# Second layer of a two-layer trunk: four of eight weight pairs with seven products in the first groups of chunks 1 and 2, and four of their banks copied aside

## The chip, the cores and the metric

The kernel runs on one core of one Trainium2 chip. The metric is the device time of one execution, in microseconds; times of several runs are given as their median. TensorE is called PE here, VectorE DVE, ScalarE ACT, GpSimd POOL, and SP is the engine that issues the loads.

## What is computed

256 tokens of width 2048 pass two layers. Each layer has attention (chunked in the first, stick-breaking in the second), a cross-attention into 256 memory tokens, an output projection, and a squared-ReLU MLP with 8192 inner features. The change is in the second layer's MLP. Of the reference this matters:

```
def sq_relu_mlp(h, g, w_in, w_out):
    return jnp.square(jax.nn.relu(rms_norm(h, g) @ w_in)) @ w_out

h = h + sq_relu_mlp(h, norm_mlp[layer], w_mlp_in[layer], w_mlp_out[layer])
```

## The kernel before

All products are made in three passes of a reduced-precision float: every operand is split into a high part `hi` and a low part `lo`, and hi*hi, hi*lo and lo*hi are summed in a PSUM bank. Weights stream from HBM in units of 128 x 1024 float32 (512 KB). SP loads a unit into `raw`; ACT casts `raw` to `hi`; DVE subtracts to get `lo`; then PE may use it. `weights()` keeps up to three units prepared ahead of the one that PE takes (`AHEAD = 3`, four `hi` and five `lo` buffers).

The MLP of a layer goes through the 8192 features in four chunks `c` of 2048 (`NCH = 4`). A chunk has two stages. The **up projection** makes the 2048 activated features of the chunk, 16 tiles of 128 features, two at a time (`two_tiles`, `up`, `finish`); DVE works on each tile after PE. The **down projection** multiplies them with the weights of the chunk and adds to sums over chunks. For chunks 0, 1 and 2 it has two groups, `pair_group(c, 0, ...)` and `pair_group(c, 1, ...)`; each makes 1024 of the 2048 output columns for both halves of the tokens, as four blocks of 128 x 512 that are called 11, 21, 12 and 22 (token half, column half).

A group goes through eight pairs of k-tiles, `j` = 0 to 7. A pair is done in one of two ways:
- with **eight products**: two units, step "1" for the column half 1 and step "2" for half 2; each is 12 matmuls of 512 columns, into banks 11 and 21, or 12 and 22. Together 24 matmuls, two casts, two subtractions.
- with **seven products** (a Strassen-Winograd scheme; `Sevenfold`, `prepare_seven`): steps 0 to 3 with 6, 3, 6 and 6 matmuls, together 21, into the four banks and four more, p1, p5, p6 and p7. Its weights are sums of the four blocks of a pair, which DVE makes in place in `raw` (steps 2 and 3: lines 222, 223, 225 and 226, each 512 wide), and every step has a cast (line 227) and a subtraction (line 228) of its own, 1024 wide except in step 1, which is 512 wide. The activations for it (`factors`, tiles `s12`, `s34`, `s_hi`, `s_lo`) are made in the up projection.

The table `SEVEN[layer][chunk][group]` lists which pairs use seven products: THREE is 0, 2, 4 and FOUR is 0, 2, 4, 6. `group_order` puts the units of the other pairs between the steps of the sevens: behind steps 1, 2 and 3 for THREE, behind steps 1 and 2 for FOUR.

When a bank is complete, `add` adds it to sums in SBUF: `d` tiles hold the four blocks of each group summed over chunks, `e` tiles the sums for p1 and p6, for p5, and for p7. Bank p1 goes into two sums, each other bank into one, so a group has nine additions of 512 columns. They are done in one of three ways: DVE adds from the bank (line 1042), ACT copies a bank that starts a sum (line 1040, chunk 0), or, where a list `staged` is given, ACT copies the bank to SBUF (line 1035) and DVE adds the copy later (line 1143). Before the change `staged` is given in the second groups of chunks 1 and 2, and in the first group of chunk 3.

PE runs its instructions in the order of the code. The other engines' instructions are put in an order by a scheduler when the kernel is built, and each engine then runs in that order, waiting at an instruction until its inputs are there.

Of the kernel before, what the change touches and what calls it, by code (L numbers as in the profile page):

```python
# [9 lines left out]
F32 = mybir.dt.float32  # L10
# [6 lines left out]
P = 128  # L17
# [7 lines left out]
NCH = FF // D  # L25
# [20 lines left out]
THREE, FOUR = (0, 2, 4), (0, 2, 4, 6)  # L46
SEVEN = [
    [(FOUR, FOUR), (THREE, FOUR), (THREE, FOUR), (THREE,)],
    [(FOUR, FOUR), (THREE, FOUR), (THREE, FOUR), (FOUR,)],
]  # L50


def group_order(sevens):


    others = [(j, col) for col in "12" for j in range(KT // 2) if j not in sevens]
    behind = (1, 2, 3) if len(sevens) == 3 else (1, 2)
    steps = []
    for j in sevens:
        for i in range(4):  # L60
            steps.append((j, i))
            if i in behind:
                steps.append(others.pop(0))
    return steps + others
# [41 lines left out]
def trunk(  # L106
# [25 lines left out]
    wide = ctx.enter_context(tc.tile_pool(name="wide", bufs=7))  # L132
# [124 lines left out]
    def weights(held=0):  # L257

        while len(prepared) < AHEAD + 1 - held and state["next"] < len(stream):
            prepare()  # L260
        return prepared.popleft()
# [6 lines left out]
    def start_side(g):  # L268
        active.append(g)
# [4 lines left out]
    def slot():  # L274
        clock["slot"] += 1
        if waiting and clock["slot"] >= max(clock["last"] + waiting[0][1], waiting[0][2]):
            active.append(waiting.popleft()[0])
            clock["last"] = clock["slot"]
        for g in list(active):
            try:  # L280
                next(g)
            except StopIteration:
                active.remove(g)
# [326 lines left out]
    def heads4(name):  # L610
        return grp.tile([P, 1024], F32, name=name, tag="g4")
# [139 lines left out]
    def new_act(name):  # L751
        return acts.tile([P, KT, 2 * T], F32R, name=name, tag="act")
# [203 lines left out]
    def mlp(l, xg_, sq, h, done):  # L956
# [4 lines left out]
        def summed(m, g):  # L961

            return sums[2 * m + g // 2][:, (g % 2) * 512 : (g % 2 + 1) * 512]
# [3 lines left out]
        def product_sum(i, n):  # L967

            return extra[i][:, n * 512 : (n + 1) * 512]

        def turned(g, then):

            for o in (4 * g, 4 * g + 2):
                yield
                tp = ps_t.tile([P, 512], F32, name="tp", tag="t")
                for i in range(2):
                    for m in range(2):
                        a = (o + i - 4 * g) * P
                        nc.tensor.transpose(
                            tp[:, i * T + m * P : i * T + (m + 1) * P],  # L980
                            summed(m, g)[:, a : a + P], ident[:],
                        )
                nc.vector.tensor_tensor(h(o, 2), tp[:], h(o, 2), op=ALU.add)  # L983
                if then is not None:
                    then(o)
                    then(o + 1)

        def merged(n):

            u, p5, p7 = (product_sum(i, n) for i in range(3))  # L990
            for i, (dst, src) in enumerate((
                (summed(0, 2 * n + 1), u),
                (summed(0, 2 * n + 1), p5),
                (u, p7),
                (summed(1, 2 * n), u),
                (u, p5),
                (summed(1, 2 * n + 1), u),
            )):
                nc.vector.tensor_tensor(dst, dst, src, op=ALU.add)
                if i % 2 == 1:  # L1000
                    yield

        def product(bank, a, w, count):

            for lhs, rhs in ((a[0], w[0]), (a[0], w[1]), (a[1], w[0])):
                mm(bank[:], lhs, rhs, count[0] == 0, count[0] == count[1] - 1)
                count[0] += 1

        def pair_group(c, n, hid, factors, staged=None):

            banks = {q: ps_mm.tile([P, 512], F32, name="acc", tag="acc") for q in ("11", "21", "12", "22")}
            banks.update((q, ps_s.tile([P, 512], F32, name="acc", tag="s")) for q in ("p1", "p5"))
            banks["p6"] = ps_t.tile([P, 512], F32, name="acc", tag="t")
            banks["p7"] = ps_y.tile([P, 512], F32, name="acc", tag="y")
            sevens = len(SEVEN[l][c][n])
            counts = {q: [0, 3 * sevens] for q in banks}
            for q in ("11", "21", "12", "22"):
                counts[q][1] = 6 * (KT // 2 - sevens) + (3 * sevens if q != "22" else 0)

            sums_of = {  # L1020
                "11": [summed(0, 2 * n)], "21": [summed(1, 2 * n)],
                "12": [summed(0, 2 * n + 1)], "22": [summed(1, 2 * n + 1)],
                "p1": [product_sum(0, n), summed(0, 2 * n)], "p6": [product_sum(0, n)],
                "p5": [product_sum(1, n)], "p7": [product_sum(2, n)],
            }

            def add(q, a, w):
                product(banks[q], a, w, counts[q])
                if counts[q][0] < counts[q][1]:
                    return  # L1030
                src = banks[q][:]
                if staged is not None and q in ("12", "22", "p1", "p5", "p6", "p7"):

                    copy = wide.tile([P, 512], F32, name="copy", tag="wide")
                    nc.scalar.copy(copy[:], src)
                    staged.extend((dst, copy[:]) for dst in sums_of[q])
                    return
                for dst in sums_of[q]:
                    if c == 0 and q not in ("11", "p6"):
                        nc.scalar.copy(dst, src)  # L1040
                    else:
                        nc.vector.tensor_tensor(dst, src, dst, op=ALU.add)

            def tokens(kt, m):
                return [hid[:, kt, i * T + m * P : i * T + (m + 1) * P] for i in range(2)]

            def part(unit, k2):
                return [x[:, k2 * 512 : (k2 + 1) * 512] for x in unit]

            for j, step in group_order(SEVEN[l][c][n]):  # L1050
                w = weights()
                if step in ("1", "2"):
                    for m in range(2):
                        for k2 in range(2):
                            add(f"{m + 1}{step}", tokens(2 * j + k2, m), part(w, k2))
                    slot()
                    continue
                s = factors[j]
                pairs = [
                    (("p1", tokens(2 * j, 0)), ("11", tokens(2 * j + 1, 0))),  # L1060
                    (("12", s[3]),),
                    (("p5", s[0]), ("p7", s[2])),
                    (("p6", s[1]), ("21", tokens(2 * j + 1, 1))),
                ][step]
                for k2, (q, a) in enumerate(pairs):
                    add(q, a, part(w, k2))
                if step in (1, 3):
                    slot()

        began = clock["slot"]  # L1070
        for c in range(NCH):
            hid = new_act(f"hid{l}_{c}")
            squares = {}
            factors = {}
# [56 lines left out]
            n = FIRST_UP if c == 0 else 0  # L1131
# [2 lines left out]
                two_tiles(xg_, [lambda b, i=i: up(i, b) for i in (f, f + 1)])  # L1134

            if c < NCH - 1:
                pair_group(c, 0, hid, factors)
                staged = None if c == 0 else []
                pair_group(c, 1, hid, factors, staged)

                def add_second(staged=staged, c=c):
                    for i, (dst, src) in enumerate(staged or ()):
                        nc.vector.tensor_tensor(dst, dst, src, op=ALU.add)
                        if i % 2 == 1:
                            yield
                    if c == NCH - 2:
                        yield from merged(1)
                        if l == 1:
                            yield from turned(3, None)

                start_side(add_second())
                continue

            staged = [] if l == 1 else None
# [21 lines left out]
            def down_early(o, bank):  # L1176
                low = low_part(bank)
                nc.gpsimd.tensor_tensor(low[:], low[:], h(o), op=ALU.add)
                nc.vector.tensor_tensor(h(o), bank[:, :T], low[:], op=ALU.add)
# [12 lines left out]
            for g in range(2, 4):  # L1192
# [3 lines left out]
                for o in range(4 * g, 4 * g + 4):  # L1196
                    if o == KT - 1:
                        last_tile(
                            hid, lambda b, o=o: down_early(o, b), lambda b, o=o: down_last(o, b)
# [97 lines left out]
    for hd in range(NH):  # L1297
        q = nar.tile([P, T], F32, name=f"qb{hd}", tag="bias", bufs=6)
# [83 lines left out]
```

## Time and profile before

| | |
|---|---|
| median of 3 runs | 2172.17 us (2171.57 to 2173.44) |
| the profiled execution, own time | 2173.2 us |
| its span in the trace | 2171.3 us |
| busy in the span | PE 2164.1, DVE 1639.0, ACT 1196.6, POOL 324.4 us |

The span is the time from the program's first instruction to its last one in the trace; the execution's own time is 1.9 us more. Busy time is the sum over an engine's instructions without overlap. A matmul's shown duration is longer than the time until the next one starts, because they are pipelined: what counts is the distance between starts. The same holds on DVE, where the next instruction starts a little before the shown end of the last.

### The profile page before, as it was taken

How to read it: one execution, taken by the hardware profiler on the slowest of the kernel's cores; microseconds unless marked ns; L12 is line 12 of the kernel's file. 1: busy time of each engine (PE TensorE's matmuls, PEld its weight loads, DVE VectorE, ACT ScalarE, POOL GpSimd, SP SyncE). 2: the span in 40 equal slices, each digit the busy share in tenths (PEclk: the TensorE clock that was granted, in tenths of full speed). 3: DMA queues.
4: the chain of work that ended last, by engine and by line, in shares of the span. 5: the costliest groups of instructions: out<-in, count | busy, mean ns of one | idle time of the engine just before them, and what ended most of it. 6: DMA issues, size and time to landing. Idle time of an engine off the chain costs nothing.

```text
span 2171.3 us, 30203 instructions
## 1 busy us (share of the span) xinstructions
PE 2164.1 (100%) x11123; PEld 1856.6 (86%) x11123; DVE 1639.0 (75%) x2239; ACT 1196.6 (55%) x1680; POOL 324.4 (15%) x349
## 2 busy tenths in 40 slices
PE   9999999999999999999999999999999999999999
PEld 8888888888888888888878888888888888888887
DVE  7765555677977987997876556567797798799796
ACT  7645545555655565555545447655565556555553
POOL 0010102621001001001041112253100100100100
PEclk9999999999999999999999999999999999999999
DMA  9655656665765765666666654455676567667664
GB/s 331 194 173 162 180 173 196 187 193 168 210 214 172 210 210 184 192 214 192 200 177 186 182 192 140 130 185 184 181 207 216 172 198 221 191 178 221 187 182 155
DMA packets 213315, 414.64 MB, mean 191 GB/s; under 512 B 13232, under 2 KB 144304, under 8 KB 213168
## 3 DMA queue, kind: packets, MB, share of 16 engines
q1 hardware_dynamic: 212592, 410.63, 62.3%
q8 instruction: 87, 1.43, 0.3%
q10 hardware_dynamic: 576, 2.10, 0.3%
q14 instruction: 60, 0.49, 0.1%
HBM read 410.58 MB, written 2.10 MB: 190 GB/s over the span
## 4 chain that ended last, share of the span: by engine, by line
PE 99%; DVE 0%; DMA 0%; ACT 0%; issue 0%; ACTq 0%
PE acc L77 94%; PE accs L77 1%; PE tp L77 1%; PE yp L77 1%; PE s L77 1%; PE z L77 1%; DMA raw<-in_w_o 0%; PE cold L77 0%; ACT hi L173 0%; DVE lo L250 0%; DVE h L983 0%; DVE lo L176 0%; DVE kvx L465 0%; ACT hi L249 0%; PE stat L77 0%
## 5 line engine op out<-in xcount | busy, mean ns | idle before, releaser
L176 DVE TENSOR_TENSOR lo<-raw,hi 128x1024 fp32r<-128x1024 f32 (+1 forms) x524 | 644.4, 1237 | 357.6 <-ACT hi L173 239.5
L173 ACT CAST hi<-raw 128x1024 fp32r<-128x1024 f32 (+1 forms) x524 | 546.7, 1045 | 380.0 <-PE acc L77 307.5
L77 PE MATMUL acc<-hi,hid 128*128 128x512 f32 x1474 | 482.4, 390 | 0.0
L77 PE MATMUL acc<-mlpx,hi 128*128 128x512 f32 x2048 | 472.6, 390 | 0.0
L77 PEld LDWEIGHTS acc<-mlpx,hi 128*128 128x128 f32 x2048 | 382.0, 188 | 77.8
L77 PEld LDWEIGHTS acc<-hi,hid 128*128 128x128 f32 x1474 | 277.4, 188 | 57.7
L77 PE MATMUL acc<-lo,hid 128*128 128x512 f32 x737 | 287.4, 390 | 0.0
L1080 POOL TENSOR_TENSOR hid<-upsq,hid 128x256 fp32r<-128x256 f32 x128 | 122.2, 963 | 1086.2 <-ACT hid L1079 1086.2
L227 ACT CAST hi<-raw 128x1024 fp32r<-128x1024 f32 x204 | 192.0, 946 | 132.8 <-PE acc L77 57.2
L77 PEld LDWEIGHTS acc<-mlpx,lo 128*128 128x128 f32 x2048 | 250.6, 192 | 2.8
L77 PE MATMUL acc<-mlpx,lo 128*128 128x256 f32 x2048 | 252.0, 283 | 0.0
L228 DVE TENSOR_TENSOR lo<-raw,hi 128x1024 fp32r<-128x1024 f32 x204 | 222.8, 1107 | 29.3 <-ACT hi L227 27.7
L249 ACT CAST hi<-raw 128x1024 fp32r<-128x1024 f32 x146 | 154.0, 1055 | 127.5 <-PE acc L77 104.0
L77 PE MATMUL acc<-hi,xg 128*128 128x512 f32 x640 | 210.5, 399 | 0.0
L250 DVE TENSOR_TENSOR lo<-raw,hi 128x1024 fp32r<-128x1024 f32 x146 | 178.4, 1222 | 16.3 <-ACT hi L249 15.6
L77 PEld LDWEIGHTS acc<-lo,hid 128*128 128x128 f32 x737 | 138.7, 188 | 28.7
L77 PEld LDWEIGHTS acc<-hi,xg 128*128 128x128 f32 x640 | 120.2, 188 | 24.6
L451 ACT COPY low<-acc 128x256 f32<-128x256 f32 x188 | 69.1, 368 | 112.5 <-PE acc L77 112.2
L77 PE MATMUL acc<-lo,xg 128*128 128x512 f32 x320 | 124.7, 390 | 0.0
L77 PE MATMUL acc<-y,hi 128*128 128x512 f32 x512 | 119.9, 391 | 0.0
L77 PEld LDWEIGHTS acc<-y,hi 128*128 128x128 f32 x512 | 95.0, 188 | 19.1
L1079 ACT CAST hid<-upsq 128x256 fp32r<-128x256 f32 x128 | 51.9, 406 | 77.1 <-DVE upsq L1078 77.1
(200 smaller groups left out, 2570.5 us busy)
## 6 DMA issues: line engine op xcount, KB each, us to landing
raw<-in_w_up SPq DMA_DIRECT2D x256, 512.0 KB, 4.4
raw<-in_w_down SPq DMA_DIRECT2D x256, 512.0 KB, 5.6
raw<-in_w_in SPq DMA_DIRECT2D x80, 512.0 KB, 3.6
raw<-in_w_o SPq DMA_DIRECT2D x64, 512.0 KB, 3.9
raw<-in_w_mem SPq DMA_DIRECT2D x28, 512.0 KB, 6.2
raw<-in_w_kv_v SPq DMA_DIRECT2D x24, 512.0 KB, 3.7
raw<-in_w_kv_k SPq DMA_DIRECT2D x24, 512.0 KB, 4.0
raw<-in_w_q SPq DMA_DIRECT2D x24, 512.0 KB, 4.2
```

Of the source, the lines that this page charges most:

```text
L77: return self._tc.keep_in_program_order(fn(*args, **kwargs))
L173: nc.scalar.copy(hi[:, :n], raw[:, :n])
L176: nc.vector.tensor_tensor(lo, raw, hi.bitcast(F32), op=ALU.subtract)
L227: nc.scalar.copy(hi4, src)
L228: nc.vector.tensor_tensor(lo4, src, hi4.bitcast(F32), op=ALU.subtract)
L249: nc.scalar.copy(hi4, turned)
L250: nc.vector.tensor_tensor(lo4, turned, hi4.bitcast(F32), op=ALU.subtract)
L451: nc.scalar.copy(low[:], bank[:, T:])
L1079: nc.scalar.copy(hid[:, f, :T], a[:])
L1080: nc.gpsimd.tensor_tensor(hid[:, f, T:], a[:], hid[:, f, :T].bitcast(F32), op=ALU.subtract)
```

## The change

In the second layer the first groups of chunks 1 and 2 use four sevens, not three. In these two groups banks p1, p5, p6 and p7 are copied by ACT into free 128 x 1024 buffers (two copies in each, named `copy1_0`, `copy1_2`, `copy2_0`, `copy2_2`), and their five additions are put on the list `staged`, with those of the second group, whose additions are written behind both groups in the code. Banks 11, 21, 12 and 22 of the first group are added by DVE from PSUM as before.

```
--- before.py
+++ after.py
@@ -46,7 +46,7 @@
 THREE, FOUR = (0, 2, 4), (0, 2, 4, 6)
 SEVEN = [
     [(FOUR, FOUR), (THREE, FOUR), (THREE, FOUR), (THREE,)],
-    [(FOUR, FOUR), (THREE, FOUR), (THREE, FOUR), (FOUR,)],
+    [(FOUR, FOUR), (FOUR, FOUR), (FOUR, FOUR), (FOUR,)],
 ]
 
 
@@ -1024,14 +1024,28 @@
                 "p5": [product_sum(1, n)], "p7": [product_sum(2, n)],
             }
 
+            spare = []
+
             def add(q, a, w):
                 product(banks[q], a, w, counts[q])
                 if counts[q][0] < counts[q][1]:
                     return
                 src = banks[q][:]
+                copy = None
                 if staged is not None and q in ("12", "22", "p1", "p5", "p6", "p7"):
-
-                    copy = wide.tile([P, 512], F32, name="copy", tag="wide")
+                    if n == 1 or c == NCH - 1:
+
+                        copy = wide.tile([P, 512], F32, name="copy", tag="wide")
+                    elif q[0] == "p":
+                        if len(spare) % 2 == 0:
+                            spare.append(heads4(f"copy{c}_{len(spare)}"))
+                        else:
+                            spare.append(spare[-1])
+                        i = (len(spare) - 1) % 2
+                        copy = spare[-1][:, i * 512 : (i + 1) * 512]
+                    else:
+                        copy = None
+                if copy is not None:
                     nc.scalar.copy(copy[:], src)
                     staged.extend((dst, copy[:]) for dst in sums_of[q])
                     return
@@ -1134,8 +1148,9 @@
                 two_tiles(xg_, [lambda b, i=i: up(i, b) for i in (f, f + 1)])
 
             if c < NCH - 1:
-                pair_group(c, 0, hid, factors)
                 staged = None if c == 0 else []
+
+                pair_group(c, 0, hid, factors, staged if l == 1 else None)
                 pair_group(c, 1, hid, factors, staged)
 
                 def add_second(staged=staged, c=c):
```

Line numbers of the changed kernel are 14 or 15 higher from `add` on: line 1042 becomes 1056, 1035 becomes 1049, 1143 becomes 1158; lines 222 to 250 stay. (In rows of the kernel before, L1158 is the addition of copies in chunk 3, in `merge_first`; there it becomes 1173.)

DVE, second layer, chunk 1, at the end of the first group, before the change. `lo691` is the subtraction for step 2 of the last of the three sevens, `lo693` that for step 3; `lo696` is the first unit of the second group; `d1_0`, `d1_2`, `e1_0`, `e1_1`, `e1_2` are sums, `acc` a bank.

```order
L228 TENSOR_TENSOR lo691_16403<-raw688_1_16356,hi691_16402 128x1024
L1042 TENSOR_TENSOR d1_0_13678<-acc_16202,d1_0_13678 128x512
L250 TENSOR_TENSOR lo692_16419<-raw692_16417,hi692_16418 128x1024
L228 TENSOR_TENSOR lo693_16427<-raw688_0_16354,hi693_16426 128x1024
L1042 TENSOR_TENSOR e1_1_13683<-acc_16207,e1_1_13683 128x512
L250 TENSOR_TENSOR lo694_16446<-raw694_16444,hi694_16445 128x1024
L1042 TENSOR_TENSOR e1_2_13684<-acc_16209,e1_2_13684 128x512
L250 TENSOR_TENSOR lo695_16460<-raw695_16458,hi695_16459 128x1024
L1042 TENSOR_TENSOR e1_0_13682<-acc_16208,e1_0_13682 128x512
L228 TENSOR_TENSOR lo696_16481<-raw696_0_16476,hi696_16480 128x1024
L1042 TENSOR_TENSOR d1_2_13680<-acc_16203,d1_2_13680 128x512
L228 TENSOR_TENSOR lo697_16493<-raw696_1_16478,hi697_16492 128x512
```

The same place in the changed kernel, where `lo695` is step 2 of the last of four sevens, `lo697` its step 3, and `lo698` and `lo699` are steps 0 and 1 of the second group's first seven.

```order
L228 TENSOR_TENSOR lo695_16448<-raw692_1_16407,hi695_16447 128x1024
L1056 TENSOR_TENSOR d1_0_13678<-acc_16202,d1_0_13678 128x512
L1158 TENSOR_TENSOR e1_0_13682<-e1_0_13682,copy1_0_16456 128x512
L250 TENSOR_TENSOR lo696_16464<-raw696_16462,hi696_16463 128x1024
L228 TENSOR_TENSOR lo697_16472<-raw692_0_16405,hi697_16471 128x1024
L1158 TENSOR_TENSOR d1_0_13678<-d1_0_13678,copy1_0_16456 128x512
L228 TENSOR_TENSOR lo698_16494<-raw698_0_16489,hi698_16493 128x1024
L1158 TENSOR_TENSOR e1_1_13683<-e1_1_13683,copy1_0_16456 128x512
L1158 TENSOR_TENSOR e1_2_13684<-e1_2_13684,copy1_2_16504 128x512
L228 TENSOR_TENSOR lo699_16507<-raw698_1_16491,hi699_16506 128x512
L1056 TENSOR_TENSOR d1_0_13678<-acc_16204,d1_0_13678 128x512
L1056 TENSOR_TENSOR d1_2_13680<-acc_16205,d1_2_13680 128x512
```

Between step 2 of the last seven and the second group's first unit there stood three units of other pairs (lo692, lo694, lo695), and one stands there now (lo696); the additions stand as close together as before, with `copy` in place of `acc` for five of them.

DVE, the following rows, before the change: `lo697` is step 1 of the second group's first seven, `lo698` a unit of another pair, `lo699` the seven's step 2, made from `raw696_1` after lines 222 and 223.

```order
L222 TENSOR_TENSOR raw696_1_16478<-raw696_1_16478 128x4x128
L250 TENSOR_TENSOR lo698_16510<-raw698_16508,hi698_16509 128x1024
L1042 TENSOR_TENSOR d1_0_13678<-acc_16204,d1_0_13678 128x512
L223 TENSOR_TENSOR raw696_1_16478<-raw696_1_16478,raw696_0_16476 128x4x128
L1042 TENSOR_TENSOR d1_2_13680<-acc_16205,d1_2_13680 128x512
L225 TENSOR_TENSOR raw696_0_16476<-raw696_1_16478,raw696_0_16476 128x4x128
L228 TENSOR_TENSOR lo699_16537<-raw696_1_16478,hi699_16536 128x1024
L226 TENSOR_TENSOR raw696_0_16476<-raw696_0_16476 128x4x128
L250 TENSOR_TENSOR lo700_16550<-raw700_16548,hi700_16549 128x1024
L228 TENSOR_TENSOR lo701_16558<-raw696_0_16476,hi701_16557 128x1024
```

The same place in the changed kernel: `lo700` is the unit of another pair, `lo701` the seven's step 2, made from `raw698_1`.

```order
L250 TENSOR_TENSOR lo700_16526<-raw700_16524,hi700_16525 128x1024
L1056 TENSOR_TENSOR d1_2_13680<-acc_16203,d1_2_13680 128x512
L1158 TENSOR_TENSOR e1_0_13682<-e1_0_13682,copy1_2_16504 128x512
L222 TENSOR_TENSOR raw698_1_16491<-raw698_1_16491 128x4x128
L223 TENSOR_TENSOR raw698_1_16491<-raw698_1_16491,raw698_0_16489 128x4x128
L225 TENSOR_TENSOR raw698_0_16489<-raw698_1_16491,raw698_0_16489 128x4x128
L226 TENSOR_TENSOR raw698_0_16489<-raw698_0_16489 128x4x128
L228 TENSOR_TENSOR lo701_16547<-raw698_1_16491,hi701_16546 128x1024
L250 TENSOR_TENSOR lo702_16560<-raw702_16558,hi702_16559 128x1024
L228 TENSOR_TENSOR lo703_16568<-raw698_0_16489,hi703_16567 128x1024
```

The four in-place sums of the second group's first seven (222, 223, 225, 226) stood between its step 1, two additions and other subtractions, with line 222 ahead of `lo698`; now they stand behind all nine additions of the first group and behind `lo700`.

ACT, the same place of chunk 1, before the change: the casts for the second group's first units.

```order
L249 CAST hi695_16459<-raw695_16458 128x1024
L227 CAST hi696_16480<-raw696_0_16476 128x1024
L227 CAST hi697_16492<-raw696_1_16478 128x512
L249 CAST hi698_16509<-raw698_16508 128x1024
L227 CAST hi699_16536<-raw696_1_16478 128x1024
L249 CAST hi700_16549<-raw700_16548 128x1024
L227 CAST hi701_16557<-raw696_0_16476 128x1024
```

The same place in the changed kernel.

```order
L227 CAST hi698_16493<-raw698_0_16489 128x1024
L1049 COPY copy1_0_16456<-acc_16207 128x512
L1049 COPY copy1_2_16504<-acc_16209 128x512
L227 CAST hi699_16506<-raw698_1_16491 128x512
L249 CAST hi700_16525<-raw700_16524 128x1024
L1049 COPY copy1_2_16504<-acc_16208 128x512
L227 CAST hi701_16546<-raw698_1_16491 128x1024
L249 CAST hi702_16559<-raw702_16558 128x1024
```

Three of the first group's four copies now stand between these casts; the cast `hi701` reads `raw698_1` after line 223 of DVE.

## Rows read from the trace of the kernel before

**Rows 1.** The page: busy time of each engine, and the chain that ended last.
```profile
PE 2164.1 (100%) x11123; PEld 1856.6 (86%) x11123; DVE 1639.0 (75%) x2239; ACT 1196.6 (55%) x1680; POOL 324.4 (15%) x349
...
PE 99%; DVE 0%; DMA 0%; ACT 0%; issue 0%; ACTq 0%
PE acc L77 94%; PE accs L77 1%; PE tp L77 1%; PE yp L77 1%; PE s L77 1%; PE z L77 1%; DMA raw<-in_w_o 0%; PE cold L77 0%; ACT hi L173 0%; DVE lo L250 0%; DVE h L983 0%; DVE lo L176 0%; DVE kvx L465 0%; ACT hi L249 0%; PE stat L77 0%
```

**Rows 2.** PE's waits in the whole span: us in total, times, longest us.
```profile
PE tp L77 <- DVE h L983: 2.7, 2, 1.9
PE cold L77 <- DVE zeros L144: 1.1, 1, 1.1
PE acc L77 <- ACT y L473: 0.2, 1, 0.2
```

**Rows 3.** PE in time, chunk 3's first group: start us, duration us, instruction.
```profile
2114.82 0.39 PE L77 MATMUL acc<-hi,s_hi 128*128 128x512 f32 x1
2115.05 0.39 PE L77 MATMUL acc<-lo,s_hi 128*128 128x512 f32 x1
...
2118.90 0.39 PE L77 MATMUL acc<-hi,s_hi 128*128 128x512 f32 x1
2119.12 0.39 PE L77 MATMUL acc<-lo,s_hi 128*128 128x512 f32 x1
```

**Rows 4.** DVE in time, the end of chunk 3's first group (four sevens).
```profile
2111.73 1.22 DVE L228 TENSOR_TENSOR lo<-raw,hi 128x1024 fp32r<-128x1024 f32 x1
2112.87 0.68 DVE L1042 TENSOR_TENSOR d<-acc,d 128x512 f32<-128x512 f32 x1
2113.47 0.68 DVE L1158 TENSOR_TENSOR e<-e,copy 128x512 f32<-128x512 f32 x1
2114.07 1.22 DVE L250 TENSOR_TENSOR lo<-raw,hi 128x1024 fp32r<-128x1024 f32 x1
2115.20 1.22 DVE L228 TENSOR_TENSOR lo<-raw,hi 128x1024 fp32r<-128x1024 f32 x1
2116.34 0.68 DVE L1158 TENSOR_TENSOR d<-d,copy 128x512 f32<-128x512 f32 x1
2116.94 1.22 DVE L250 TENSOR_TENSOR lo<-raw,hi 128x1024 fp32r<-128x1024 f32 x1
```

**Rows 5.** DVE in time, chunk 0's first group: in-place sums that follow each other.
```profile
1604.75 0.69 DVE L222 TENSOR_TENSOR raw<-raw 128x512 f32<-128x512 f32 x1
1605.48 0.69 DVE L223 TENSOR_TENSOR raw<-raw,raw 128x512 f32<-128x512 f32 x1
```

**Rows 6.** DVE in time, chunk 1, around the second group's first seven.
```profile
1778.06 0.68 DVE L223 TENSOR_TENSOR raw<-raw,raw 128x512 f32<-128x512 f32 x1
...
1779.94 1.22 DVE L228 TENSOR_TENSOR lo<-raw,hi 128x1024 fp32r<-128x1024 f32 x1
1781.09 0.68 DVE L226 TENSOR_TENSOR raw<-raw 128x512 f32<-128x512 f32 x1
1781.69 1.22 DVE L250 TENSOR_TENSOR lo<-raw,hi 128x1024 fp32r<-128x1024 f32 x1
```

**Rows 7.** ACT and PE in time, the same place: cast and first uses.
```profile
1778.86 1.05 ACT L227 CAST hi<-raw 128x1024 fp32r<-128x1024 f32 x1 [2.57 <-DVE raw L223]
...
1782.74 0.39 PE L77 MATMUL acc<-lo,s_hi 128*128 128x512 f32 x1
```

**Rows 8.** Groups by line, whole span: count, busy us, mean ns, idle before.
```profile
L1042 DVE TENSOR_TENSOR e<-acc,e 128x512 f32<-128x512 f32 x24 | 16.4, 685 | 2.1 <-PE acc L77 2.1
L1143 DVE TENSOR_TENSOR e<-e,copy 128x512 f32<-128x512 f32 x16 | 10.6, 683 | 0.0
L1035 ACT COPY copy<-acc 128x512 f32<-128x512 f32 x30 | 17.1, 586 | 2.9 <-PE acc L77 2.9
```

**Rows 9.** PE in time, end of the first layer's MLP: a wait and what follows.
```profile
1111.11 0.66 PE L77 MATMUL tp<-ident,d 128*128 128x128 f32 x4 [1.91 <-DVE h L983]
...
1112.64 0.63 PE L77 MATMUL acc<-lo,hid 128*128 128x512 f32 x1
...
1115.63 0.50 PE L77 MATMUL acc<-hi,hid 128*128 128x512 f32 x1
1115.97 0.60 PE L77 MATMUL tp<-ident,d 128*128 128x128 f32 x4
```

**Rows 10.** Windows (PE, PEld, DVE, ACT, POOL busy; granted clock; DMA): these waits, chunk 3's first group.
```profile
1112.50:1116.00 3.50, 3.50 (x10) 2.60 (x10) 3.50 (x5) 0.91 (x2) 3.50 (x6) 0.52 0.53 150
...
2146.00:2149.00 3.00, 2.21 (x19) 1.89 (x18) 2.15 (x3) 1.04 (x1) 0.00 (x0) 1.00 0.19 62
...
2078.00:2119.00 41.00, 41.00 (x183) 33.94 (x182) 40.06 (x49) 26.05 (x31) 2.96 (x2) 1.00 0.71 191
```

## The prediction

> **What bounds the kernel now.** I read the page first: PE is busy for 2164.1 of 2171.3 us, and the chain that ended last is PE's for 99%, nearly all of it matmuls into `acc` banks [rows 1]. Since a busy PE could still be a stretched one, the list of PE's waits comes next. It holds 4.0 us in the whole span: 1.1 at the start, and 2.7 in two waits for DVE where the MLPs' last sums are turned [rows 2]. None lies in the groups that the change touches. PE in time shows how dense it runs: two equal instructions that are 18 matmuls apart start 4.08 us apart (2114.82 to 2118.90), so a matmul of 512 columns takes 0.2265 us of PE's time, whatever its shown duration of 0.39 says [rows 3]. Time can therefore change in two ways: fewer matmuls, or waits that are not there now. DVE's margin decides the second. In chunk 3's first group, which already has four sevens behind an up projection and copies of its banks by ACT, DVE is busy for 40.06 of 41.00 us [rows 10], and ACT for 26.05. DVE is the engine that has nothing to give.
>
> **What is removed.** Two pairs go from 24 to 21 matmuls: 6 x 0.2265 = 1.36 us of PE time, all on the path. That is the whole possible gain, 0.06%. The time must move by more than 0.2%, 4.3 us, to be told from no change in a measurement of this kernel.
>
> **What is added inside the two first groups.** Each fourth seven replaces two units of 1024. Over a group that is 1.5 casts more on ACT (3.5 for 2) and 1.5 subtractions and four in-place sums more on DVE. Whether PE waits inside the group needs no sum: chunk 3's first group has the same order of pairs and of DVE's instructions up to its last seven, and no wait of PE stands there [rows 2]. I cost this part at nothing; the cover is DVE's lead. At that group's last seven, the subtraction for step 2 starts at 2111.73, ends at 2112.95 and is used at 2115.05 [rows 3, 4]: a lead of 2.1 us, which the first groups of chunks 1 and 2 should show as well. The four copies are 4 x 0.586 us on ACT [rows 8], in a group where it has 15 us free. They cost nothing there, unless a cast stands behind one at a wrong moment.
>
> **Where the five additions go.** The code writes them behind both groups. The order of the built program shows that the scheduler puts them where they were: all nine additions of the first group stand between step 2 of its last seven and step 2 of the second group's first seven. And a copy in SBUF is no cheaper for DVE than a bank: 683 ns against 685 [rows 8]. So DVE's work in this passage is not lightened. What changes is the passage. With three sevens PE has 69 matmuls to go through between these two steps, four units of 12 among them; with four sevens it has 45, two units of 12 among them. The same additions must be done in 24 matmuls, 5.4 us, less.
>
> [...]
>
> **The passage worked out**, with time 0 at the start on DVE of the last seven's step 2 subtraction (`lo695`). The first six instructions stand in the same order in chunk 3, so I take their starts from there: subtraction, two additions, two subtractions, one addition, and the next may start at 2116.94 - 2111.73 = 5.21 [rows 4]. From the same rows, each 1024-wide subtraction then takes 1.13 until the next start, each 512-wide instruction 0.60. In the new order follow `lo698` (1.13), two additions (1.20), `lo699` (512 wide, 0.60), two additions (1.20), `lo700` (1.13), two additions (1.20): 11.67. Then line 222, which line 223 must wait for: 0.73 from start to start [rows 5], and 0.69 for line 223 to end: **13.1**. Only now can ACT cast `raw698_1`. In chunk 1 before the change this cast starts 0.12 behind the end of line 223 (1778.06 + 0.68, 1778.86) and takes 1.05 [rows 6, 7]: 14.3. PE's first matmul with it is due 44 matmuls after the use of `lo695`, which comes 2115.05 - 2111.73 = 3.32 in [rows 3, 4]: 3.32 + 44 x 0.2265 = 13.3. **PE waits 1.0 us for the cast.** Its next matmul needs `lo701`, which on DVE stands behind lines 225 and 226: 13.1 + 0.05 + 0.73 (226 waits for 225 as 223 for 222) + 0.60 + 1.22 = 15.7, due at 13.3 + 0.23 + the 1.0 of the wait = 14.5. **PE waits 1.2 us more.** That is 2.2 us for a passage, ended by ACT's cast at line 227 and DVE's subtraction at line 228. Before the change the same subtraction ended at about 1781.16 for a use at 1782.74 [rows 6, 7]: 1.6 us to spare.
>
> From below a passage costs 1.4 us: if the additions' starts are 0.06 closer and the lead 0.3 more than in chunk 3. From above 2.8, with hand-overs of 0.1 to 0.2 us at each of the three changes of engine. I take 2.2, since every term has its own row. After it the next subtraction is there just in time (15.7 + 1.13 = 16.8 against a use at 15.7 + 5 x 0.2265 + 0.23 = 17.1), and further on the order is that of the second groups before, which show no waits. Chunks 1 and 2 have the same order, so there are two passages: 4.4 us.
>
> **The clock.** [...] From 1112.64 to 1115.63, seven matmuls took 2.99 us and not 1.59, 1.4 us more, and the matmuls at both edges add some 0.1 each. A wait of under 0.8 us at 2146 left the clock at 1.00 [rows 10]. [...] I take a fall of the clock behind each, at 1.5 us: 3.0 us. The bounds are none and 3.2.
>
> **Sum.** -1.36 + 4.4 + 3.0 = +6.0 us. The profiled execution had 2173.2 us, 1.0 above the median of 2172.17, and would become 2179.2; from the median it is **2178.2 us**, 0.28% slower.
>
> **The rivals.**
> - *The waits come, and the clock falls once, or not at all.* The new wait is split in two, and each half alone is nearer to the harmless 0.8. With one fall 2176.7, with none 2175.2: the latter is within 0.2%.
> - *No wait: the additions are out of the way, as the change's words say.* This ends on the other side: PE keeps running and 6 matmuls are gone, 2170.8 us, not slower. The mechanism would be a lead of DVE at the last seven of 4.3 us, not 2.1; that is the point from which it decides. For it: in other places of these groups ACT and DVE do idle for some tenths of a microsecond, and DVE's lead is taken from another chunk. Against it: the additions stand in the passage by the built order, and the lead can't build up while DVE is 98% busy.
> - *More waits.* If ACT's copies hold a bank that the second group starts with, or the DVE backlog outlives the first seven, a second wait of about 1 us in each passage gives 2180.2. Against it: p1 is copied several microseconds ahead of its next use, and the sum above catches up by the next unit.
>
> **Chances.** Both waits with two falls 0.45, with one 0.22, with none 0.13; no wait 0.13; more waits 0.05; something else that gains 0.02. The range from 2174.8 to 2179.4 takes in the first three cases, 0.80, with the bounds of the passage in part. Slower by over 0.2% (above 2176.5) are the first and the last but one, and some 0.13 of the single fall, which lies on the edge: 0.63. Faster by over 0.2% would need 4.3 us where the change can give 1.4: 0.02. Within 0.2%: 0.35.
>
> **What would show it.** In the changed kernel's list of PE's waits: two of about 1.0 us for ACT's cast at line 227 and two of about 1.2 us for DVE's subtraction at line 228, one pair in chunk 1 near 1782 us, where the same step stands now [rows 7], and one a chunk later, each behind step 1 and one unit of the second group. The five additions (now line 1158, `copy`) should stand in DVE's timeline just ahead of them, not in the up projection, at 0.68 us each. The first groups should end 0.7 us earlier than before. The granted clock should read about 0.5 for some 3.4 us behind each pair; if it stays at 1.00, the third term is wrong. If PE shows no wait there, the lead was mis-sized; if it waits inside the first group, the comparison with chunk 3 was wrong.

## The result, and the profile after

The changed kernel takes **2179.3 us** (median of 9 runs, 2176.53 to 2180.63), the kernel before in the same 9 rounds 2172.68 us. The ratio is **1.0028**, 95% interval 1.002 to 1.0037: slower by 0.28%, and clear of no change. The forecast was 2178.2 us, 0.28% slower, with a range from 2174.8 to 2179.4: the median lies inside it by 0.1 us.

The profiled execution of the changed kernel took 2177.9 us; its span and PE's busy time on the page, and PE's list of waits over the whole span (us in total, times, longest us), answer to [rows 1, 2]:

```profile
span 2176.2 us, 30218 instructions
...
PE 2165.2 (99%) x11117; PEld 1856.0 (85%) x11117; DVE 1649.0 (76%) x2251; ACT 1202.8 (55%) x1692; POOL 324.2 (15%) x349
```

```profile
PE tp L77 <- DVE h L983: 2.7, 2, 1.9
PE acc L77 <- DVE lo L228: 1.9, 2, 0.9
PE acc L77 <- ACT hi L227: 1.6, 2, 0.9
PE cold L77 <- DVE zeros L144: 1.1, 1, 1.1
PE acc L77 <- ACT y L473: 0.3, 1, 0.3
```

PE has 6 matmuls fewer, and two new lines among its waits, each twice: one for ACT's cast of a seven's unit (line 227), one for DVE's subtraction (line 228). Half of them stand here, in chunk 1 of the second layer. PE in time:

```profile
1769.89 0.39 PE L77 MATMUL acc<-lo,s_hi 128*128 128x512 f32 x1
...
1779.41 0.39 PE L77 MATMUL acc<-lo,hid 128*128 128x512 f32 x1
1779.63 0.39 PE L77 MATMUL acc<-hi,hid 128*128 128x512 f32 x1
1780.87 0.50 PE L77 MATMUL acc<-hi,s_hi 128*128 128x512 f32 x1 [0.85 <-ACT hi L227]
1782.31 0.50 PE L77 MATMUL acc<-lo,s_hi 128*128 128x512 f32 x1 [0.93 <-DVE lo L228]
...
1783.26 0.63 PE L77 MATMUL acc<-lo,s_hi 128*128 128x512 f32 x1
...
1786.24 0.68 PE L77 MATMUL acc<-hi,hid 128*128 128x512 f32 x2
```

A wait is read from starts, since the idle time in brackets begins only when the modelled end of the last matmul is past. From 1779.63 to 1780.87 are 1.24 us, one matmul of 0.23 and a wait of 1.01; from 1780.87 to 1782.31 are 1.44 us, one matmul and a wait of 1.21. Together 2.22 us. Then seven matmuls, from 1783.26 to 1786.24, take 2.98 us in place of 1.59.

DVE in time at the same place, and ACT's cast, answer to [rows 4 to 7]:

```profile
1766.57 1.22 DVE L228 TENSOR_TENSOR lo<-raw,hi 128x1024 fp32r<-128x1024 f32 x1
...
1777.06 0.68 DVE L1056 TENSOR_TENSOR d<-acc,d 128x512 f32<-128x512 f32 x1
1777.66 0.68 DVE L1158 TENSOR_TENSOR e<-e,copy 128x512 f32<-128x512 f32 x1
1778.26 0.68 DVE L222 TENSOR_TENSOR raw<-raw 128x512 f32<-128x512 f32 x1
1778.97 0.69 DVE L223 TENSOR_TENSOR raw<-raw,raw 128x512 f32<-128x512 f32 x1
1779.70 0.69 DVE L225 TENSOR_TENSOR raw<-raw,raw 128x512 f32<-128x512 f32 x1
1780.43 0.69 DVE L226 TENSOR_TENSOR raw<-raw 128x512 f32<-128x512 f32 x1
1781.04 1.22 DVE L228 TENSOR_TENSOR lo<-raw,hi 128x1024 fp32r<-128x1024 f32 x1
```

```profile
1779.78 1.04 ACT L227 CAST hi<-raw 128x1024 fp32r<-128x1024 f32 x1 [4.30 <-DVE raw L223]
```

DVE never pauses in this stretch. Counted from the start of the last seven's step 2 subtraction at 1766.57, line 223 ends at 13.09 (the prediction's sum: 13.1), the cast at 14.25 (14.3), the subtraction that PE waits for at 15.69 (15.7). PE's first use of the last seven's step 2 is the matmul at 1769.89, 3.32 behind that start, as in chunk 3 [rows 3, 4].

The windows of the same execution (PE, PEld, DVE, ACT, POOL busy; granted clock; DMA) answer to [rows 10]:

```profile
1779.50:1782.80 3.30, 1.52 (x6) 0.73 (x5) 3.23 (x5) 3.02 (x4) 0.00 (x0) 1.00 0.34 93
1783.00:1786.30 3.30, 3.30 (x10) 2.56 (x9) 3.27 (x5) 1.28 (x2) 0.00 (x0) 0.50 0.63 155
...
1957.10:1960.40 3.30, 3.30 (x9) 2.59 (x8) 3.30 (x4) 1.57 (x3) 0.00 (x0) 0.50 0.53 143
```

In the first, PE is busy for less than half; in the second it is busy throughout, at a granted clock of 0.50; the third is the same place in chunk 2. With one matmul in 0.227 us at the full clock and 0.426 at half (2.98 us for seven), eight matmuls in such a stretch cost 1.6 us more.

### The profile page after: what moved, and what is told of

It is laid out like the page before. It is cut to its first block, busy times and chain, and to the rows that moved or that the text cites. A ratio compares the mean times of both kernels' runs of the same rounds, so it can differ in the third digit from the quotient of the medians.

```text
span 2176.2 us, 30218 instructions
## 1 busy us (share of the span) xinstructions
PE 2165.2 (99%) x11117; PEld 1856.0 (85%) x11117; DVE 1649.0 (76%) x2251; ACT 1202.8 (55%) x1692; POOL 324.2 (15%) x349
## 4 chain that ended last, share of the span: by engine, by line
PE 97%; DVE 2%; issue 0%; ACT 0%; DMA 0%; SPq 0%; DVEq 0%; ACTq 0%
PE acc L77 93%; PE accs L77 1%; PE tp L77 1%; PE yp L77 1%; PE s L77 1%; PE z L77 1%; DVE lo L250 0%; DVE lo L228 0%; DVE d L1056 0%; DVE e L1158 0%; ACT hi L249 0%; DMA raw<-in_w_mem 0%; ACT hi L173 0%; DVE h L983 0%; DVE lo L176 0%
## 5 line engine op out<-in xcount | busy, mean ns | idle before, releaser
L77 PE MATMUL acc<-hi,hid 128*128 128x512 f32 x1454 | 477.6, 390 | 0.0
L228 DVE TENSOR_TENSOR lo<-raw,hi 128x1024 fp32r<-128x1024 f32 x212 | 231.1, 1107 | 27.5 <-ACT hi L227 25.9
L250 DVE TENSOR_TENSOR lo<-raw,hi 128x1024 fp32r<-128x1024 f32 x142 | 174.8, 1232 | 14.7 <-ACT hi L249 13.9
```

The lines of the kernel that those rows point to most:

```text
L77: return self._tc.keep_in_program_order(fn(*args, **kwargs))
L228: nc.vector.tensor_tensor(lo4, src, hi4.bitcast(F32), op=ALU.subtract)
L250: nc.vector.tensor_tensor(lo4, turned, hi4.bitcast(F32), op=ALU.subtract)
```

## The experiments

The theory to test was that the nine additions, 5.4 us of DVE time that still stand between the last seven's step 2 and the next first seven's step 2, make DVE 2.2 us late there, because the fourth seven took 24 matmuls out of that passage; and that the clock falls behind the wait. Rival A was that ACT's copies delay the casts; rival B that the fourth seven overloads DVE whatever becomes of the additions.

**Additions really in the up projection.** `pin` holds an instruction behind what its engine has been given until then.

```
-                        nc.vector.tensor_tensor(dst, dst, src, op=ALU.add)
+                        pin(nc.vector.tensor_tensor(dst, dst, src, op=ALU.add), l == 1 and i < 5)
```

> The change, with the five additions of each first group held behind what DVE has been given until then, so that they really stand in the next up projection. Theory (the nine additions crowd the shortened passage between the last seven's step 2 and the second group's first step 2, DVE is 2.2 us late there, and the clock falls behind the wait): five additions of 0.60 us leave the passage, 3.0 us against 2.2 us of lateness; PE waits there for neither cast nor subtraction, the granted clock stays at 1.00 in both second groups, and the time is 6 matmuls below the kernel before: about 2171.3 against 2172.7, -1.4 us. Rival A (ACT's copies delay the casts): the copies stay, so the waits stay, about +6 us. Rival B (the fourth seven alone overloads DVE): the waits stay, and new ones may come in the up projection, +4 to +8 us.

Measured: 2171.52 us (2170.84 to 2173.15, 11 runs) against 2172.94, ratio 0.9995 (0.9986 to 1.0004). Of PE's waits from the second layer's MLP to the end one is left, at the kernel's end:

```profile
PE tp L77 <- DVE h L983: 0.8, 1, 0.8
```

The median moved by -1.4 us, but the interval can't tell this from no change, and the six matmuls are not all of it: the traces, compared at the end of this section, show -0.5 us. DVE's order shows the additions ahead of and between the first subtractions of the up projection (line 176):

```profile
1814.22 1.22 DVE L176 TENSOR_TENSOR lo<-raw,hi 128x1024 fp32r<-128x1024 f32 x1
1815.35 1.29 DVE L1158 TENSOR_TENSOR e<-e,copy 128x512 f32<-128x512 f32 x2
1816.56 1.22 DVE L176 TENSOR_TENSOR lo<-raw,hi 128x1024 fp32r<-128x1024 f32 x1
1817.69 1.29 DVE L1158 TENSOR_TENSOR d<-d,copy 128x512 f32<-128x512 f32 x2
```

The fourth seven and the copies are all there, and the waits of 2.2 us are gone: A and B both fall as their cause.

**Copies alone.**

```
-    [(FOUR, FOUR), (FOUR, FOUR), (FOUR, FOUR), (FOUR,)],
+    [(FOUR, FOUR), (THREE, FOUR), (THREE, FOUR), (FOUR,)],
```

> The copies of the change without the fourth seven: three sevens in both first groups, banks p1, p5, p6 and p7 copied by ACT. Theory: the passage keeps its 69 matmuls, DVE's additions stand in it as before at the same 0.68 us each, no wait, no change: within 0.3 us of the kernel before. Rival A (copies delay casts): a wait of some tenths of a us to 1 us for ACT's cast in both second groups, +1 to +5 us with the clock. Rival B: no change.

Measured: 2173.08 us against 2172.94, ratio 1.0002 (0.9993 to 1.001), no wait of PE in the down projections. By themselves the copies bring nothing there. The trace has one new wait of 0.3 us for DVE's `h` (line 983) at 2025 us, in the next up projection.

**The fourth seven alone**, which is the kernel before with the table row of the change.

```
-    [(FOUR, FOUR), (THREE, FOUR), (THREE, FOUR), (FOUR,)],
+    [(FOUR, FOUR), (FOUR, FOUR), (FOUR, FOUR), (FOUR,)],
```

> The fourth seven of the change without the copies: DVE adds all nine banks from PSUM, as before. Theory: DVE has the same instructions in the passage, so PE waits about 2.2 us in each of the two second groups, perhaps in other portions since a bank can be late as well as a cast; the time is that of the changed kernel within 1 us, +5 to +7 us against before. If copies help by freeing banks: waits over 3 us. Rival A (the copies are the cause): no wait, -1.4 us. Rival B (the fourth seven alone): +5 to +7 us too.

Measured: 2175.6 us (2174.64 to 2176.43, 11 runs) against 2172.94, ratio 1.0013 (1.0004 to 1.0022). This is less than expected: +2.7 us in the median (+3.3 in the traces), not +5 to +7. PE in time at the same place, and the window behind it:

```profile
1777.48 0.39 PE L77 MATMUL acc<-hi,hid 128*128 128x512 f32 x1
1778.11 0.50 PE L77 MATMUL acc<-lo,hid 128*128 128x512 f32 x1 [0.24 <-DVE lo L250]
...
1780.51 0.39 PE L77 MATMUL acc<-hi,hid 128*128 128x512 f32 x1
1781.19 0.50 PE L77 MATMUL acc<-hi,s_hi 128*128 128x512 f32 x1 [0.29 <-ACT hi L227]
1782.62 0.50 PE L77 MATMUL acc<-lo,s_hi 128*128 128x512 f32 x1 [0.93 <-DVE lo L228]
```

```profile
1783.00:1786.40 3.40, 3.40 (x17) 2.79 (x16) 3.40 (x4) 1.61 (x3) 0.00 (x0) 1.00 0.59 139
```

The waits, again from starts less one matmul, are 0.40, 0.45 and 1.20: 2.05 us, nearly the sum of the changed kernel, but with eleven matmuls between the first and the second. Behind them the clock stayed at 1.00, in chunk 2 too. DVE's lateness is nearly the same without the copies; the clock's fall is not. In the built order of this kernel one more addition stands ahead of the unit in front of the passage's end, so the unit is late as well.

**The five additions left out** (the second layer's sums lack them).

```
                     for i, (dst, src) in enumerate(staged or ()):
+                        if l == 1 and i < 5:
+                            continue
```

> The change with the five copied additions of each first group left out altogether (ten additions in all, so part of the second layer's down projection is missing from the output); the copies and the fourth seven stay. Theory: as with the additions held back, no wait at the passage, -1.4 us against before; what this gains over the kernel with the additions in the up projection is what they cost there, which should be under 0.2 us. Rival A: waits stay, +6 us. Rival B: waits stay, +4 to +6 us.

Measured: 2171.85 us (2170.3 to 2172.83) against 2172.94, ratio 0.9994 (0.9985 to 1.0003), no wait in the list. The median moved by -1.1 us. What the additions cost in the up projection is 0.3 us by the traces of this and the first experiment, and lost in the noise of the times.

**The five additions on POOL.**

```
+                        adder = nc.gpsimd if l == 1 and i < 5 else nc.vector
-                        nc.vector.tensor_tensor(dst, dst, src, op=ALU.add)
+                        adder.tensor_tensor(dst, dst, src, op=ALU.add)
```

> The change with the five additions of each first group given to POOL, which has nothing to do in the down projections; the copies and the fourth seven stay. Theory: what counts is DVE's time in the passage; without the five additions there the wait is gone wherever they go, the clock stays, -1.4 us against the kernel before. A rival form of it: POOL's additions slow DVE's neighbouring instructions, since some DVE instructions that ran beside POOL took 1.7 us in place of 1.2 in the trace before; then part of the wait comes back, 0.5 to 1 us a passage, and the time is within 1 us of before.

Measured: 2178.92 us (2178.0 to 2181.93, 6 runs) against 2172.27, ratio 1.0033 (1.002 to 1.0045). My expectation failed, and its rival form was too mild. Groups by line from 1768 to 1777 us (count, busy us, mean ns), and PE's waits from the second layer's MLP on:

```profile
L1159 POOL TENSOR_TENSOR e<-e,copy 128x512 f32<-128x512 f32 x4 | 8.0, 2026 | 23.9 <-ACT copy L1049 23.9
L228 DVE TENSOR_TENSOR lo<-raw,hi 128x1024 fp32r<-128x1024 f32 (+1 forms) x4 | 7.5, 1903 | 0.0
...
L250 DVE TENSOR_TENSOR lo<-raw,hi 128x1024 fp32r<-128x1024 f32 x1 | 1.7, 1726 | 0.0
...
L1056 DVE TENSOR_TENSOR d<-acc,d 128x512 f32<-128x512 f32 x2 | 1.4, 679 | 0.0
```

```profile
PE acc L77 <- DVE lo L250: 4.4, 2, 2.2
PE acc L77 <- DVE d L1056: 0.7, 2, 0.3
```

While POOL adds, DVE's subtractions take 1.7 to 1.9 us in the mean, where they took 1.22 and less in [rows 4, 6]; the additions from a bank kept their 0.68 us. What leaves DVE as instructions comes back as longer ones: in each passage PE waits 2.2 us for a unit (2.34 from starts, 1777.94 to 1780.51), and just ahead of it 0.3 us for DVE's addition from a bank (line 1056). Why the subtractions get longer beside POOL, no run here shows.

**Chunk 1 only.**

```
-    [(FOUR, FOUR), (FOUR, FOUR), (FOUR, FOUR), (FOUR,)],
+    [(FOUR, FOUR), (FOUR, FOUR), (THREE, FOUR), (FOUR,)],
```

> The change in chunk 1 alone: four sevens and copies there, three sevens (and the copies) in chunk 2. Theory: one pair of waits, 1.0 and 1.2 us, near 1780 us, and none in chunk 2; 3 matmuls saved: -0.7 + 2.2 = +1.5 us without a fall of the clock, +3.0 with one, so half of what the whole change costs. A rival, that a part of the change's cost lies elsewhere than in the passages (the up projections, the end): less than half or more than half, by over 1 us.

Measured: 2174.98 us (2173.4 to 2178.07, 11 runs) against 2172.27, ratio 1.0012 (1.0004 to 1.0021): +2.7 us, about half of what the whole change costs. The profile has one pair of waits with one fall of the clock behind it, and none in chunk 2.

**Three of the five additions** (the last two, for p7 and p6, are left out of the output's sums).

```
                     for i, (dst, src) in enumerate(staged or ()):
+                        if l == 1 and i in (3, 4):
+                            continue
```

> The change with the last two of the five copied additions left out in each first group (the sums for p6 and p7 lack these groups' part in the output). Theory, by the sum of the prediction with two additions of 0.60 us less: line 223 ends at 11.9, the cast at 13.1 and in time for 13.3, the subtraction lo701 at 14.5 against 13.5: one wait of 1.0 us for DVE in each passage, none for ACT. The clock should stay, as it did behind the 0.8 us wait at the kernel's end: 2 x 1.0 - 1.4 = +0.6 us. If the clock falls behind 1.0 us as well, +2 to +4 us.

Measured: 2173.37 us (2172.15 to 2174.03) against 2172.27, ratio 1.0004 (0.9995 to 1.0012). PE waits once in a passage, and only for DVE:

```profile
1780.55 0.39 PE L77 MATMUL acc<-hi,s_hi 128*128 128x512 f32 x1
1781.66 0.50 PE L77 MATMUL acc<-lo,s_hi 128*128 128x512 f32 x1 [0.73 <-DVE lo L228]
```

From starts this is 0.9 us (expected: 1.0), with the granted clock at 1.00 behind it. Beside the four additions from banks, five additions in the passage make 2.2 us of waits, three 0.9, none 0.

**The changed kernel again**, without an edit, for the spread of its times: nine timed executions, one of them profiled, and three more profiled ones.

> The changed kernel once more, for another execution's clock and for the spread of its times. Theory: the waits are the same to 0.1 us in every execution, and what differs between executions is the clock alone: it falls behind both passages or behind neither, and some executions show more than one stretch at half clock behind a passage, which would account for the times above 2179 us. A rival: the waits themselves differ from execution to execution by a microsecond or more.

> The changed kernel, one more profiled execution. The waits so far were the same to 0.1 us, and the clock fell behind both passages in one execution (2177.9 us) and behind the second alone in another (2177.2 us). Theory: an execution's time is about 2174.7 us, which is the kernel before without any fall of its clock plus 3.1 us, and 1.5 us for each stretch of 3.4 us at half clock, wherever it lies; so an execution above 2179 us has three or more of them, among them that at the end of the first layer's MLP. A rival: it has longer waits.

> As the look before: 2174.7 us and 1.5 us for each stretch at half clock, with the same waits; a rival has longer waits in the slower executions.

> As the two looks before: 2174.7 us and 1.5 us for each stretch at half clock, with the same waits; a rival has longer waits in the slower executions.

Measured, timed: 2177.2 us (2176.58 to 2179.77, 9 runs) against 2172.27, ratio 1.0025 (1.0015 to 1.0035). The five profiled executions of this kernel took 2177.9, 2177.2, 2177.76, 2180.51 and 2177.84 us. In all five the two new lines of PE's waits read 1.9 and 1.6 or 1.7: the waits don't vary. The clock does: behind the two passages it fell in both, the second alone, both, both, and the first alone. In the fourth and the fifth it fell at the end of the first layer's MLP too. The slowest execution has three such stretches; its windows:

```profile
1113.00:1116.40 3.40, 3.40 (x9) 2.67 (x8) 3.40 (x5) 0.91 (x2) 3.40 (x5) 0.50 0.40 154
1785.50:1788.80 3.30, 3.30 (x9) 2.58 (x8) 3.30 (x4) 1.42 (x2) 0.00 (x0) 0.50 0.58 146
1959.60:1962.90 3.30, 3.30 (x9) 2.52 (x9) 3.30 (x4) 1.72 (x3) 0.00 (x0) 0.50 0.65 145
```

By 2174.7 us and 1.5 a stretch, three executions with two stretches come to 2177.7 and took 2177.76 to 2177.9. The one with one stretch took 2177.2 for 2176.2, and has a wait of 0.9 us for a cast of ACT near 11 us, where the others show 0.5 at most. The one with three took 2180.51 for 2179.2; its window from 4 to 7.1 us, first below, has five matmuls fewer than that of the execution of 2177.9 us, second, which is 1.1 us of delay at the start:

```profile
4.00:7.10 3.10, 3.04 (x12) 2.55 (x11) 1.84 (x5) 1.26 (x3) 0.00 (x0) 1.00 0.89 321
```

```profile
4.00:7.10 3.10, 3.05 (x17) 2.46 (x16) 1.99 (x5) 1.25 (x3) 0.00 (x0) 1.00 0.83 277
```

So the spread between these executions is the clock and the first loads, not the waits. The timed executions fit: over the 13 profiled executions of all kernels here, a mean granted clock of 1.000 goes with no stretch at half clock, 0.999 with one, 0.998 with two and 0.997 with three. By this, of the change's 18 timed executions eight had one stretch, ten had two or three, and none had none. Which executions show a fall behind a passage, with the same wait in front of it, stays open.

**The same stretch in every trace.** The medians take in what lies ahead of the change: the first loads, and the clock at the end of the first layer's MLP, which fell in 5 of the 13 profiled executions behind a wait of 1.9 us that all 13 have. So the traces are compared over the second layer's MLP alone, from the start of PE's `inv<-mlpsq` there (1489.61 us in the kernel before) to the start of its last group of matmuls, `acc<-hid,lo` (2166.07):

| kernel | us | against before | stretches at half clock in it |
|---|---|---|---|
| before | 676.46 | | 0 |
| the change, three executions | 683.26 to 683.30 | +6.8 | 2 |
| the change, two executions | 681.66, 681.69 | +5.2 | 1 |
| additions in the up projection | 675.96 | -0.5 | 0 |
| copies alone | 676.88 | +0.4 | 0 |
| fourth seven alone | 679.77 | +3.3 | 0 |
| five additions left out | 675.65 | -0.8 | 0 |
| five additions on POOL | 685.36 | +8.9 | 2 |
| chunk 1 only | 680.01 | +3.6 | 1 |
| three of five | 677.09 | +0.6 | 0 |

Executions of the change with as many stretches agree to 0.04 us, and a stretch costs 1.6 us. Without the five additions in the passage the gain is 0.5 to 0.8 us, not 1.36. The first groups do end 0.68 us earlier each, but PE loses 0.28 us again in each second group: with the additions in the up projection three of its matmuls start at 1791.39, 1791.79 and 1792.13, behind a subtraction of DVE that ends at 1791.74. Such a delay is too short for the list of waits. What else is lost lies in chunk 3's up projection and was not followed further.

## Why the prediction was right

**Removed work.** Right for the matmuls: 11117 for 11123, and 0.68 us gained by the end of each first group. Not all of it reaches the end: the two kernels without the additions in the passage gain 0.5 and 0.8 us in the traces. Their medians moved by -1.4 and -1.1 us, and by their intervals (0.9986 to 1.0004 and 0.9985 to 1.0003) this is not told from none.

**No cost inside the first groups.** Right: no wait of PE stands in them.

**Where the additions go, and their price.** Right: five additions of line 1158 stand in the passage, and DVE's time for one is what it was from a bank. One addition takes as long on DVE with a copy as from a bank (0.68 us shown, 0.60 from start to start, at 1777.66 and 1777.06).

**The passage worked out.** Right to some hundredths of a microsecond, term by term, as the rows of after show, and the lead at its start was that of chunk 3 to the same precision. That DVE's additions in a passage that the fourth seven has shortened are the cause of the waits is shown from five sides: the additions taken out, moved back and reduced to three, and the additions kept with the fourth seven alone (waits) and with the copies alone (none).

**The clock.** Right in size: 1.6 us a stretch for 1.5. That a fall would come was a chance taken, and the row behind it was weaker than it looked: the granted clock of 0.52 behind a wait of 1.9 us [rows 9, 10] is from one execution, and behind the same wait the clock stayed at 1.00 in 8 of the 13 profiled ones. The forecast of a fall behind each passage holds in three of the change's five profiled executions; in the other two it fell behind one.

**The sum.** Over the second layer's MLP it came to +6.8 us with two falls, for a forecast of +6.0. Each passage costs some 0.25 us more than was summed, 0.1 of it in the first matmul behind the waits (0.34 us from 1782.31 to 1782.65) and 0.1 in the clock; the rest lies in chunk 3's up projection. That the medians came out at 2179.3 and, timed again, at 2177.2 us is in part luck: the execution at the first median shows a mean granted clock of 0.997, so three stretches by the count above, and the one at the second 0.999, one stretch, where the sum had two.

**What it did not see.** "They cost nothing there", of the copies, is right inside the first groups. But without them the same lateness of DVE comes in three portions, and the kernel with the fourth seven alone took 2175.6 us (1.0004 to 1.0022), against 1.002 to 1.0037 and 1.0015 to 1.0035 for the change. The intervals of the ratios overlap a little. Of that kernel there is one profile, in which the clock fell behind neither passage, but its 11 timed executions bear it out: six show a mean granted clock of 1.000 and five 0.999, so none has two stretches, about as in the kernel before (14 and 19 of 33). As far as these runs go, the clock falls behind most of the passages with the copies and behind none or few without them. That the shape of the wait does it, two portions for three, is not shown: the sum of the waits differs too (2.22 for 2.05 us), and with the same two portions four of the 11 timed executions of the kernel with chunk 1 only show 1.000.

The version with the additions held back has the lowest median of those that compute everything, 2171.52 us, though not clear of the kernel before. The same in the first layer was not tried: there `h`, `d`, `e` and the second layer's memory keys and values hold all 13 of the buffers that the copies would need.

## What to carry to other kernels

When work is cut from the engine that bounds, the stretch in which the other engines must finish theirs gets shorter: sum that work by the built order of the instructions, from one use to the next, not by where the code writes it. Work that is said to be deferred is deferred only if something holds it back. And a wait of the bounding engine can have a second price, the clock behind it, which comes in some executions and not in others (here 1.6 us a stretch, behind eight of the ten passages in the change's five profiled executions): compare the same stretch of the traces before reading a difference of medians as the effect of an edit.

## What was not expected of the hardware

POOL's additions of 512 columns took some 2.0 us in the mean, up to 2.3, and slowed DVE's subtractions beside them from 1.22 to 1.7 us and more, so that an idle engine's help cost more than it gave. And waits of 0.40, 0.45 and 1.20 us, in one profiled execution, left TensorE's granted clock at 1.00, where 1.01 and 1.21 us with one matmul between them were followed by 0.50 behind eight of ten passages of the change, and a single wait of 1.9 us in 5 executions of 13.
